# A decoder layer on one TensorE: end phase on plain loads, earlier operand loads, chores spread in steps, and POOL arithmetic moved to VectorE

## The chip, the cores and the metric

The kernel runs on one core of one Trainium2 chip. The metric is the device time of one launch in microseconds (us), as the median of several runs; a lower number is better. One further execution was recorded by the hardware profiler. Engines carry their short names: PE is TensorE (matmuls, and PEld its weight loads), DVE is VectorE, ACT is ScalarE, POOL is GpSimd, SP is SyncE, which only issues transfers. Each engine takes its instructions strictly in order.

## The reference, cut to what matters

One layer of width 1024 over 2048 positions, all in float32. One input projection gives six groups of 1024 columns; eight retention heads and four pooling windows use them, SiLU gates multiply both, and one output projection follows, with an RMSNorm before and one behind.

```python
h = rms_norm(x, pre_g)
proj = jnp.einsum('bsd,df->bsf', h, w_in)
q, k, v, g_ret, u, g_pool = jnp.split(proj, N_PROJ, axis=-1)
y_ret = retention_branch(q, k, v, positions, ret_norm_g) * jax.nn.silu(g_ret)
y_pool = pooling_branch(u, pool_w, pool_scale) * jax.nn.silu(g_pool)
y = jnp.concatenate([y_ret, y_pool], axis=-1)
y = jnp.einsum('bsf,fd->bsd', y, w_out)
return x + rms_norm(y, post_g)
```

Inside `retention_branch`, q and k are rotated by their position (`t1*cos - t2*sin`, `t1*sin + t2*cos`), then attention runs in chunks of 128 with a decaying state. `pooling_branch` takes running means over 2, 4, 8 and 16 positions and multiplies each group of 256 channels by `pool_w`.

## The kernel before, in words

**Products.** The large products are done by a 2x2 block scheme with seven block products instead of eight (sums S1 to S4 on the streamed side, made-up blocks on the resident side, and corrections on the result). Each float32 operand is split into an upper part (ACT, a copy that rounds) and a lower part (a subtraction), and three matmuls (upper x upper, upper x lower, lower x upper) stand for one. So one `Unit` is 7 products x 4 blocks x 3 = 84 matmuls of 128x512.

**Phases.** `line` lists 62 units in four phases: phase 0 the projections of rows 0 to 1023 (8 heads with a `qk` and a `vg` unit each, 8 `up` units for pooling), phase 1 the same for rows 1024 to 2047, phase 2 the first half of the output projection (`o0_0`, `o2_0`, ..., partial sums stored to the DRAM tensor `part`), phase 3, the end phase, its second half (`o0_8`, `o2_8`, ...), where `part` is added, the RMSNorm is taken, `x` is added and the rows go out. The first two units are written out by hand in `first`, which also takes the RMSNorm statistics of rows 0 to 1023 and builds the rotation tables.

**Order of the work.** A unit has seven steps (`at` 0 to 6, products 6, 2, 5, 7, 1 of the next unit, 4, 3). After each step `slot()` runs what `later(i, ...)` put i steps ahead, then a chore of the table `chores` starts if one stands at (phase, unit, step), and then the next unit's operands are prepared (`prep`) and the unit after that is loaded (`load`, at step 6). Chores are background work for later phases: `fold_pool_weights` (multiplies pool_w into the weights of `u`: operands split, 48 small matmuls, results stored), `stats_next`, `tables`, `combine_h` and `combine_o`. Within this program order the framework's scheduler settles each engine's queue.

**What the steps below touch.** A streamed load puts S1 and S3 in SBUF by a plain load from SP and an accumulating DMA from POOL on top of it, and the blocks 11, 12, 22 by plain loads (L254 to L268). `rope` (L420) rotates: two ACT copies swap the halves into `sw`, DVE multiplies by cos, POOL multiplies `sw` by sin (L431), DVE adds. `halves` (L753) splits the fold's operands with the lower part on POOL. In the end phase (`out_unit`) `total` copies or forms a result tile `ot`, adds `part` to it by an accumulating DMA from POOL (L686), squares it two steps later (L681), and `finish` normalises, adds `x` by an accumulating DMA (L732) and issues the store to `out` from SP (L733). Only the last unit fetches `part` by plain loads ahead (`fetch`, L673) and corrects with POOL (`adjust`, L677). Temporary tiles `T` (16 buffers of 128x528) are shared by all of this; streamed tiles `X` have 13 buffers.

Of the kernel before, what the change touches and what calls it, by code (L numbers as in the profile page):

```python
# [15 lines left out]
P = 128  # L16
# [65 lines left out]
def layer_kernel(ctx: ExitStack, tc: tile.TileContext, x, xt, pos, wt, wut, wo, pw, cols, postg, const, out):  # L82
# [126 lines left out]
    def combine_tile(n, j, b11, b12, b21, b22, keep):  # L209

        s = slice((j % 2) * BLK, (j % 2 + 1) * BLK)

        def put(p, t):
            nc.gpsimd.dma_start(out=made[n, p][j // 2][:, s], in_=t)

        def op(p, a, b, alu):
            t = T(f"c{n}{p}{j}")[:, :BLK]
            nc.vector.tensor_tensor(out=t, in0=a, in1=b, op=alu)
            put(p, t)
            return t  # L220
        if keep:
            for p, t in ((1, b11), (2, b21), (3, b22)):
                put(p, t)
        t1 = op(5, b11, b12, ALU.subtract)
        t2 = op(6, b22, t1, ALU.add)
        op(7, b12, b22, ALU.subtract)
        op(4, b21, t2, ALU.subtract)

    def combine_h(j, b0, b1):
# [4 lines left out]
        for name, b, k in (("b11", b0, j), ("b12", b1, j), ("b22", b1, KH + j), ("b21", b0, KH + j)):  # L234
            nc.vector.scalar_tensor_tensor(out=t[name], in0=t[name], scalar=col[:, k:k + 1], in1=rb[b],
                                           op0=ALU.mult, op1=ALU.mult)
        combine_tile(1, j, t["b11"], t["b12"], t["b21"], t["b22"], True)

    def combine_o(n, j):
# [5 lines left out]
        combine_tile(n, j, t["b11"], t["b12"], t["b21"], t["b22"], False)  # L245


    class Unit:
        def __init__(self, name, quads, uses):
            self.name, self.quads, self.uses = name, quads, uses  # L250
            self.op, self.bank = {}, {}
            self.fetch = self.adjust = None

        def load(self):  # L254
            self.raw = {}

            def land(name, q):
                t, view = X(f"{name}_{self.name}"), self.quads[q]
                dst = t if len(view.shape) == 2 else t.rearrange("p (f t) -> p f t", f=KH)
                nc.sync.dma_start(out=dst, in_=view)  # L260
                self.raw[name] = t
                return dst
            s1 = land("S1", "21")
            s3 = land("S3", "11")
            nc.gpsimd.dma_start(out=s1, in_=self.quads["22"], accum_op=ALU.add)
            nc.gpsimd.dma_start(out=s3, in_=self.quads["21"], accum_op=ALU.add)
            for q in ("11", "12", "22"):
                land(q, q)  # L268
# [11 lines left out]
        def prep(self, i):  # L280
            raw = self.raw
            if i == 0:
                self.add("S2", raw["S1"], raw["11"], nc.vector)
            elif i == 1:
                self.split(1, "11")
            elif i == 2:
# [10 lines left out]
            elif i == 8:  # L297
                self.split(3, "S4")

        def product(self, p, r):  # L300
# [20 lines left out]
            elif p == 6:  # L321
                nc.vector.tensor_tensor(out=o, in0=o, in1=self.x1, op=ALU.subtract)
                self.u2 = T(f"u2_{n}")[:, :BLK]
                nc.scalar.copy(out=self.u2, in_=o)  # L324
                if self.adjust:
                    self.adjust("12", self.u2)
            elif p == 2:
                self.uses["11"](o, True)
            elif p == 5:
                self.x5 = T(f"x5_{n}")[:, :BLK]  # L330
                nc.scalar.copy(out=self.x5, in_=o)
                if self.adjust:
                    self.adjust("22", self.x5)
# [21 lines left out]

    def stats_rows(b, tiles):
        ss = sml.tile([P, 2 * CPB], F32, name=f"ss{b}", tag="ss", bufs=4)
        for st in range(CPB):
            for j in range(2):
                r = tiles(st, j)  # L360
                nc.sync.dma_start(out=r, in_=x[b * BLK + st * P:b * BLK + (st + 1) * P, j * BLK:(j + 1) * BLK])
                nc.scalar.activation(out=r, in_=r, func=AF.Square, accum_out=ss[:, 2 * st + j:2 * st + j + 1])
        return ss

    def row_sums(b, ss):
        v = sml.tile([P, CPB], F32, name=f"rs{b}", tag="rs")
        s2 = ss.rearrange("p (s j) -> p s j", j=2)
        nc.vector.tensor_tensor(out=v, in0=s2[:, :, 0], in1=s2[:, :, 1], op=ALU.add)
        return v
# [30 lines left out]
    def tables(b):  # L400
        pi = T(f"pos{b}")[:, :BLK].bitcast(I32)
        nc.sync.dma_start(out=pi, in_=pos[:, b * BLK:(b + 1) * BLK].broadcast_to([P, BLK]))
        ang, kk = T(f"ang{b}")[:, :BLK], T(f"kk{b}")[:, :BLK]
        for step in angles(pi, ang, kk):
            step()
        cs, sn = T(f"cd{b}")[:, :BLK], T(f"sd{b}")[:, :BLK]
        nc.scalar.activation(out=sn, in_=ang, func=AF.Sin, scale=cst[:, C_SGN:C_SGN + 1])
        nc.scalar.activation(out=kk, in_=ang, func=AF.Abs)
        nc.scalar.activation(out=cs, in_=kk, func=AF.Sin, scale=-1.0, bias=cst[:, C_HPI:C_HPI + 1])
        for i, t in enumerate((cs, sn)):  # L410
            nc.gpsimd.dma_start(out=tabd[b][:, i, :], in_=t)
# [6 lines left out]
    held = []  # L418

    def rope(c, in_psum, b, name):  # L420
# [10 lines left out]
        nc.gpsimd.tensor_tensor(out=sw, in0=sw, in1=tabs[b][1], op=ALU.mult)  # L431
# [216 lines left out]
    def out_unit(s, f0, last, final=False):  # L648
# [26 lines left out]
        def adjust(q, t):  # L675

# [462 lines left out]
```

## Time and profile before

| what | value |
|---|---|
| median of 3 runs | 1624.98 us (1624.18 to 1631.08) |
| profiled execution, its own time | 1622.46 us |
| its span from first to last instruction | 1620.6 us |
| mean granted TensorE clock, share of full speed | 0.967 |
| PE / DVE / ACT / POOL busy, share of the span | 91% / 64% / 45% / 31% |
| DMA over the span | 243.80 MB, 150 GB/s on average |

The table gives averages over stages with different limits. The sections below read it stage by stage: in a stretch of the span, its length less PE's busy time is PE's idle time, and a granted clock under 1.00 says that part of the busy time ran at the lower of TensorE's two levels (1.2 instead of 2.4 GHz), where a matmul takes twice as long.

### The profile page before, as it was taken

The page shows a single profiled execution, that of the slowest core. Times are in us where ns is not written, and L with a number is a line of the kernel's source. Part 1 is how long each engine was busy: PE and PEld are TensorE (multiplying, and loading weights), DVE is VectorE, ACT ScalarE, POOL GpSimd, SP SyncE. Part 2 cuts the span into 40 slices and gives each one's busy share as a digit, 9 for nine tenths or more (in the row PEclk, how much of TensorE's full clock was granted, in tenths as well). Part 3 has the DMA queues.
Part 4 walks back from the last instruction along what each step waited for, and adds up shares of the span by engine and source line. Part 5 has one row for each costly group of instructions (what it writes and reads, how often), then busy time and mean ns, then how long its engine had stood idle before and what let it go on. Part 6 is the DMA issues. An engine that isn't in the chain of part 4 may idle for free. (4 is left out here: it accounts for less than half of the span.)

```text
span 1620.6 us, 20953 instructions
## 1 busy us (share of the span) xinstructions
PE 1473.8 (91%) x6976; PEld 1209.9 (75%) x6976; DVE 1044.2 (64%) x2166; ACT 722.6 (45%) x1383; POOL 500.0 (31%) x529
## 2 busy tenths in 40 slices
PE   4998979898989999799999999999996999987875
PEld 3777767687878888588888887887885888766664
DVE  6983736775757766876777667677677544645354
ACT  5554535445344434454444444344444433533331
POOL 0223231325252425522223314233245221133333
PEclk9999999999999999799999999999998999998987
DMA  8134544546454546544455535554456655887976
GB/s 309 41 78 124 150 111 109 151 131 173 140 155 133 162 123 173 180 116 105 117 156 149 161 82 148 144 162 108 121 153 191 177 155 144 286 194 149 221 163 175
DMA packets 115372, 243.80 MB, mean 150 GB/s; under 512 B 14016, under 2 KB 14144, under 8 KB 115264
## 3 DMA queue, kind: packets, MB, share of 16 engines
q1 hardware_dynamic: 75264, 149.12, 28.3%
q0 software_dynamic: 40000, 93.35, 26.4%
q8 instruction: 55, 0.90, 0.2%
q14 instruction: 53, 0.43, 0.1%
HBM read 187.88 MB, written 54.53 MB: 150 GB/s over the span
## 5 line engine op out<-in xcount | busy, mean ns | idle before, releaser
L312 PE MATMUL b_o<-rh,h_o 128*128 128x512 f32 x192 | 82.9, 432 | 40.3 <-ACT u_o L324 24.6
L431 POOL TENSOR_TENSOR sw_q<-sw_q,sin 128x512 f32<-128x512 f32 x32 | 50.6, 1583 | 144.7 <-ACT sw_q L429 98.8
L312 PE MATMUL b_up<-rh,h_up 128*128 128x512 f32 x192 | 78.7, 410 | 18.0 <-DVE gp L336 13.4
L443 POOL DMA_DIRECT2D yd<-sg x32 | 25.0, 780 | 196.3 <-DVE r L487 145.1
L312 PE MATMUL b_qk<-rh,h_qk 128*128 128x512 f32 x180 | 74.3, 413 | 10.7 <-DVE rot_k L336 5.6
L313 PE MATMUL b_o<-rl,h_o 128*128 128x512 f32 x192 | 81.2, 423 | 0.5 <-DVE rl L145 0.5
L314 PE MATMUL b_o<-rh,l_o 128*128 128x512 f32 x192 | 80.7, 420 | 0.0
L517 ACT ACTIVATE on<-op,sh,y_o 128x128 f32<-128x128 f32 x128 | 48.1, 456 | 72.7 <-DVE sh L514 72.7
L312 PEld LDWEIGHTS b_o<-rh,h_o 128*128 128x128 f32 x192 | 39.4, 205 | 54.8 <-ACT u_o L324 27.5
L313 PE MATMUL b_up<-rl,h_up 128*128 128x512 f32 x192 | 77.5, 404 | 0.0
L314 PE MATMUL b_up<-rh,l_up 128*128 128x512 f32 x192 | 77.4, 403 | 0.0
L313 PE MATMUL b_qk<-rl,h_qk 128*128 128x512 f32 x180 | 72.6, 403 | 0.0
L312 PE MATMUL b_vg<-rh,h_vg 128*128 128x512 f32 x180 | 72.3, 402 | 0.2 <-DVE rot_q L430 0.2
L314 PE MATMUL b_qk<-rh,l_qk 128*128 128x512 f32 x180 | 72.3, 402 | 0.0
L314 PE MATMUL b_vg<-rh,l_vg 128*128 128x512 f32 x180 | 70.5, 392 | 0.0
L313 PE MATMUL b_vg<-rl,h_vg 128*128 128x512 f32 x180 | 70.3, 391 | 0.0
L624 POOL TENSOR_TENSOR w<-ub 128x527 f32<-128x527 f32 x32 | 41.3, 1290 | 86.8 <-issue 41.1
L624 POOL TENSOR_TENSOR w<-w 128x525 f32<-128x525 f32 (+2 forms) x48 | 66.5, 1386 | 2.4
L145 DVE TENSOR_TENSOR rl<-m,rh 128x1024 fp32r<-128x1024 f32 x42 | 57.3, 1369 | 15.3 <-ACT rh L144 13.5
L431 POOL TENSOR_TENSOR sw_k<-sw_k,sin 128x512 f32<-128x512 f32 x32 | 49.8, 1557 | 56.1 <-ACT sw_k L429 53.0
L312 PEld LDWEIGHTS b_up<-rh,h_up 128*128 128x128 f32 x192 | 37.7, 197 | 28.8 <-DVE gp L336 15.3
L661 POOL DMA_DIRECT2D part<-pt_o x32 | 17.6, 552 | 108.9 <-ACT pt_o L349 65.7
(507 smaller groups left out, 4820.1 us busy)
## 6 DMA issues: line engine op xcount, KB each, us to landing
m<-made SPq DMA_DIRECT2D x30, 512.0 KB, 6.0
made<-c POOLq DMA_DIRECT2D x48, 256.0 KB, 4.0
yd<-sg POOLq DMA_DIRECT2D x32, 256.0 KB, 2.8
S_up<-in_wt POOLq DMA_DIRECT2D x32, 256.0 KB, 5.6
yd<-mx POOLq DMA_DIRECT2D x32, 256.0 KB, 2.8
b<-in_wo SPq DMA_DIRECT2D x32, 256.0 KB, 4.0
S_o<-yd SPq DMA_DIRECT2D x32, 256.0 KB, 4.0
S_o<-yd POOLq DMA_DIRECT2D x32, 256.0 KB, 5.9
```

Source lines behind the costliest of these rows:

```text
L145: (eng or nc.vector).tensor_tensor(out=r32(lo), in0=val, in1=hi, op=ALU.subtract)
L312: nc.tensor.matmul(o, wh, mh, start=opens and j == 0, stop=False, **more)
L313: nc.tensor.matmul(o, wh, ml, start=False, stop=False, **more)
L314: nc.tensor.matmul(o, wl, mh, start=False, stop=j == KH - 1, **more)
L431: nc.gpsimd.tensor_tensor(out=sw, in0=sw, in1=tabs[b][1], op=ALU.mult)
L443: nc.gpsimd.dma_start(out=yd[b][:, :, f, :], in_=t.rearrange("p (c t) -> p c t", c=CPB))
L517: nc.scalar.activation(out=self.on[:, c], in_=op[:, c], func=AF.Identity, scale=rs[:, i:i + 1], bias=shift[:, i:i + 1])
L624: nc.gpsimd.tensor_tensor(out=dst[:, s0:], in0=src[:, s0:], in1=src[:, s0 - step:E - step], op=ALU.add)
L661: nc.gpsimd.dma_start(out=place(part, q), in_=t)
```

## The change

- **End phase.** All eight units of phase 3 now do what the last one did: `fetch` loads their four quarters of `part` by plain loads on SP while the unit before runs. `taken` replaces the two ACT copies u2 and x5 by a DVE subtraction of `part`; the two results that come straight from PSUM get `part` by a DVE addition. The 28 accumulating DMAs from `part` and the two `adjust` steps on POOL are gone; the square is taken at once; the store to `out` is issued four steps after the accumulating DMA of `x`.
- **Streamed loads.** S1 and S3 are loaded at step 4, 11 and 22 at step 5, 12 at step 6, in place of all at step 6; the sum S2 = S1 + 11 moves from step 0 to step 1, behind the split of 11.
- **Chores.** `fold_pool_weights`, `stats_next`, `tables` and the `combine` chores issue their loads, splits, products and stores in separate steps (`later`), and the table places them elsewhere.
- **Beginning.** The first row tile of x is loaded first; the positions come as 128 full rows; the weights' upper and lower parts are split in separate steps.
- **From POOL to DVE.** The sin multiplication of the 64 rotations and the 20 lower parts of the folds.

```diff
     def combine_tile(n, j, src, keep):
...
+            t = src[p] = T(f"c{n}{p}{j}")[:, :BLK]
+            nc.vector.tensor_tensor(out=t, in0=src[a], in1=src[b], op=alu)
+            later(1, lambda: put(p, t))
...
+        def land(self, name, q, more=None):
+            t, view = X(f"{name}_{self.name}"), self.quads[q]
+            dst = t if len(view.shape) == 2 else t.rearrange("p (f t) -> p f t", f=KH)
+            nc.sync.dma_start(out=dst, in_=view)
+            if more:
+                nc.gpsimd.dma_start(out=dst, in_=self.quads[more], accum_op=ALU.add)
+            self.raw[name] = t
+
+        def load_sums(self):
+            self.raw = {}
+            self.land("S1", "21", "22")
+            self.land("S3", "11", "21")
...
         def prep(self, i):
             raw = self.raw
-            if i == 0:
-                self.add("S2", raw["S1"], raw["11"], nc.vector)
-            elif i == 1:
+            if i == 1:
+                h11 = raw["11"]
                 self.split(1, "11")
+                self.add("S2", raw["S1"], h11, nc.vector)
...
+        def taken(self, q, o, name):
+
+            t = T(f"{name}_{self.name}")[:, :BLK]
+            if self.part:
+                nc.vector.tensor_tensor(out=t, in0=o, in1=self.part[q], op=ALU.subtract)
+            else:
+                nc.scalar.copy(out=t, in_=o)
+            return t
...
-                self.u2 = T(f"u2_{n}")[:, :BLK]
-                nc.scalar.copy(out=self.u2, in_=o)
-                if self.adjust:
-                    self.adjust("12", self.u2)
+                self.u2 = self.taken("12", o, "u2")
...
-        nc.gpsimd.tensor_tensor(out=sw, in0=sw, in1=tabs[b][1], op=ALU.mult)
+        nc.vector.tensor_tensor(out=sw, in0=sw, in1=tabs[b][1], op=ALU.mult)
...
         def total(q):
-            def use(c, i):
-                o[q] = landed(c, i, f"ot{q}_{n}")
-                nc.gpsimd.dma_start(out=o[q], in_=place(part, q), accum_op=ALU.add)
...
-        def total_last(q):
             def use(c, i):
                 t = o[q] = T(f"ot{q}_{n}")[:, :BLK]
                 if i:
                     nc.vector.tensor_tensor(out=t, in0=c, in1=parts[q], op=ALU.add)
                 else:
                     c(t)
...
-                nc.sync.dma_start(out=out[spot], in_=t)
...
+                if final:
+                    nc.sync.dma_start(out=out[spot], in_=t)
+                else:
+                    later(4, lambda t=t, spot=spot: nc.sync.dma_start(out=out[spot], in_=t))
...
-        split(hi, lo, val, nc.gpsimd)
+        split(hi, lo, val)
...
     def fold_pool_weights(g):
-        pool = halves(f"p{g}", load_pool(g))
-        for dh in range(2):
-            fold_store(g, dh, fold_products(g, dh, pool, fold_split(g, dh, load_fold(g, dh))))
...
+        later(2, begin)
+        later(3, lambda: operands(0))
+        later(6, lambda: multiply(0))
+        later(7, lambda: fold_store(g, 0, st[0]))
+        later(7, second)
+        later(10, lambda: operands(1))
+        later(13, lambda: multiply(1))
+        later(14, lambda: fold_store(g, 1, st[1]))
...
             if i in upper:
                 split_w(*upper[i])
...
-    chores = {(0, 4, 0): lambda: fold_pool_weights(0), (0, 6, 0): lambda: fold_pool_weights(1),
-              (0, 12, 0): lambda: fold_pool_weights(2), (0, 15, 0): lambda: fold_pool_weights(3),
-              (0, 5, 0): lambda: stats_next(2), (0, 7, 0): lambda: stats_next(3),
-              (0, 8, 0): lambda: tables(2), (0, 9, 0): lambda: tables(3),
+    chores = {(0, 4, 0): lambda: fold_pool_weights(0), (0, 10, 0): lambda: fold_pool_weights(1),
+              (0, 14, 3): lambda: fold_pool_weights(2), (0, 16, 4): lambda: fold_pool_weights(3),
+              (0, 6, 0): lambda: stats_next(2), (0, 7, 3): lambda: stats_next(3),
+              (0, 12, 1): lambda: tables(2), (0, 13, 2): lambda: tables(3),
...
+    for j, u in enumerate(((8, 6), (18, 5), (19, 5), (20, 5))):
+        chores[(0, *u)] = lambda j=j: combine_h(j, 2, 3)
...
+                if n + 2 < len(line):
+                    ahead = line[n + 2][2]
+                    if at == 4:
+                        ahead.load_sums()
+                    elif at == 5:
+                        ahead.load_rest(("11", "22"))
+                    elif at == 6:
+                        ahead.load_rest(("12",))
```

**SP's queue in the end phase.** The first rows are those of before, from the middle of phase 3; `o4_8` runs, `o2_8` is the unit before it and `o8_8` the unit two ahead; `ot..` are its four results, `S1`, `S3`, `11`, `12`, `22` the streamed loads.

```order
L733 DMA out_0<-ot11_o2_8_13169 128x512
L733 DMA out_0<-ot22_o2_8_13241 128x512
L260 DMA S1_o8_8_13489<-yd2_91 128x512
L733 DMA out_0<-ot21_o2_8_13281 128x512
L733 DMA out_0<-ot12_o2_8_13302 128x512
L260 DMA S3_o8_8_13491<-yd2_91 128x512
L260 DMA 11_o8_8_13495<-yd2_91 128x512
L260 DMA 12_o8_8_13497<-yd2_91 128x512
L260 DMA 22_o8_8_13499<-yd2_91 128x512
```

The same place of the change, one unit earlier (`o2_8` runs, `o0_8` is before it, `o6_8` two ahead, `pt..` are the quarters of `part` for the next unit `o4_8`):

```order
L680 DMA pt11_o4_8_13265<-part4_97 128x512
L680 DMA pt22_o4_8_13267<-part5_98 128x512
L680 DMA pt21_o4_8_13269<-part5_98 128x512
L680 DMA pt12_o4_8_13271<-part4_97 128x512
L261 DMA S1_o6_8_13279<-yd1_90 128x512
L261 DMA S3_o6_8_13282<-yd1_90 128x512
L261 DMA 11_o6_8_13304<-yd1_90 128x512
L261 DMA 22_o6_8_13306<-yd1_90 128x512
L726 DMA out_0<-ot11_o0_8_13019 128x512
L726 DMA out_0<-ot22_o0_8_13065 128x512
L726 DMA out_0<-ot21_o0_8_13117 128x512
L726 DMA out_0<-ot12_o0_8_13140 128x512
```

S3, 11 and 22 stood behind the stores of the unit before; now they and S1 stand ahead of them, and only 12, the next row, stands behind. Four loads of `part` are new ahead of S1.

**POOL's queue in the end phase.** Before, one unit's stretch (`L686` adds `part`, `L732` adds `x`, `L265` and `L266` complete S1 and S3):

```order
L686 DMA ot22_o4_8_13425<-part5_98 128x512
L265 DMA S1_o8_8_13489<-yd2_91 128x512
L686 DMA ot21_o4_8_13465<-part5_98 128x512
L266 DMA S3_o8_8_13491<-yd2_91 128x512
L686 DMA ot12_o4_8_13486<-part4_97 128x512
L686 DMA ot11_o6_8_13537<-part6_99 128x512
L732 DMA ot11_o4_8_13353<-in_x 128x512
L732 DMA ot22_o4_8_13425<-in_x 128x512
L732 DMA ot21_o4_8_13465<-in_x 128x512
L732 DMA ot12_o4_8_13486<-in_x 128x512
```

The change:

```order
L722 DMA ot11_o2_8_13177<-in_x 128x512
L722 DMA ot22_o2_8_13245<-in_x 128x512
L722 DMA ot21_o2_8_13297<-in_x 128x512
L722 DMA ot12_o2_8_13320<-in_x 128x512
L263 DMA S1_o8_8_13463<-yd2_91 128x512
L263 DMA S3_o8_8_13466<-yd2_91 128x512
```

A unit has six accumulating transfers where it had ten, and no result of the running unit stands ahead of S1 and S3 any more.

**PE's queue at a fold.** Before, the third fold's first products (`p2h`, `p2l` the parts of pool_w, `w200..`, `w201..` those of the weights; `a_vg5_0` belongs to a unit):

```order
L774 MATMUL wf2_01_3529<-p2l_3501,w200h_3508 128x256
L775 MATMUL wf2_00_3516<-p2h_3500,w200l_3509 128x256
L775 MATMUL wf2_01_3529<-p2h_3500,w200l_3509 128x256
L312 MATMUL a_vg5_0_3674<-b11h0_271,h1_vg5_0_3625 128x512
L313 MATMUL a_vg5_0_3674<-b11l0_273,h1_vg5_0_3625 128x512
L773 MATMUL wf2_00_3516<-p2h_3500,w201h_3512 128x256
```

The change, the same fold:

```order
L764 MATMUL wf2_00_4233<-p2h_4129,w200h_4151 128x256
L765 MATMUL wf2_00_4233<-p2l_4130,w200h_4151 128x256
L766 MATMUL wf2_00_4233<-p2h_4129,w200l_4152 128x256
L764 MATMUL wf2_00_4233<-p2h_4129,w201h_4155 128x256
L765 MATMUL wf2_00_4233<-p2l_4130,w201h_4155 128x256
L766 MATMUL wf2_00_4233<-p2h_4129,w201l_4156 128x256
```

The fold's products stood in pieces as their operands were made, with unit matmuls between; now each result's twelve stand in one run.

## Rows read from the trace of the kernel before

**Rows 1.** The page's first part: busy us, share, instructions of each engine.

```profile
PE 1473.8 (91%) x6976; PEld 1209.9 (75%) x6976; DVE 1044.2 (64%) x2166; ACT 722.6 (45%) x1383; POOL 500.0 (31%) x529
```

**Rows 2.** Stretches of the span: length, busy per engine (x), PEclk, DMA share, GB/s.

```profile
0.00:40.00 40.00, 18.63 (x61) 12.20 (x62) 25.97 (x63) 21.96 (x39) 0.20 (x4) 1.00 0.84 313
40.00:100.00 60.00, 56.95 (x270) 46.08 (x269) 56.82 (x87) 33.58 (x53) 13.42 (x11) 1.00 0.24 51
...
140.00:265.00 125.00, 109.98 (x565) 90.53 (x565) 63.72 (x164) 62.88 (x137) 38.33 (x38) 0.95 0.47 129
265.00:485.00 220.00, 202.68 (x1011) 168.03 (x1010) 143.51 (x328) 98.83 (x197) 78.27 (x83) 0.98 0.51 144
485.00:637.00 152.00, 149.86 (x743) 125.13 (x742) 109.06 (x231) 66.93 (x135) 53.90 (x59) 1.00 0.49 138
637.00:718.00 81.00, 69.44 (x291) 55.77 (x290) 64.44 (x76) 40.31 (x67) 37.70 (x31) 0.89 0.61 178
718.00:1186.00 468.00, 460.43 (x2329) 385.62 (x2328) 321.30 (x742) 211.10 (x405) 138.16 (x146) 1.00 0.49 130
1186.00:1264.00 78.00, 63.91 (x260) 50.74 (x259) 59.76 (x71) 36.95 (x66) 36.58 (x34) 0.91 0.61 184
1264.00:1378.00 114.00, 114.00 (x503) 94.10 (x502) 49.69 (x75) 43.30 (x74) 22.46 (x35) 1.00 0.56 154
...
1421.00:1607.00 186.00, 151.42 (x587) 119.35 (x585) 82.59 (x186) 61.87 (x136) 60.34 (x68) 0.90 0.81 182
```

**Rows 3.** Waits in 1421:1607: who for whom, us in total, times, longest.

```profile
DVE sS_o L272 <- DMA S_o<-yd: 46.2, 6, 10.3
```

**Rows 4.** DMA queues and issues in 1421:1607: share of 16 engines; us to landing.

```profile
q0 software_dynamic: 9648, 17.57, 56.5%
q1 hardware_dynamic: 8851, 16.12, 23.8%
...
ot_o<-in_x POOLq DMA_DIRECT2D x28, 256.0 KB, 5.8
out<-ot_o SPq DMA_DIRECT2D x28, 256.0 KB, 5.2
ot_o<-part POOLq DMA_DIRECT2D x26, 256.0 KB, 6.4
S_o<-yd POOLq DMA_DIRECT2D x12, 256.0 KB, 5.7
S_o<-yd SPq DMA_DIRECT2D x10, 256.0 KB, 5.1
```

**Rows 5.** One stretch of 20 us where phase 2 meets phase 3.

```profile
1380.00:1400.00 20.00, 17.87 (x78) 14.15 (x77) 13.41 (x17) 10.74 (x17) 3.95 (x6) 1.00 0.94 307
```

**Rows 6.** PE's waits over the whole span.

```profile
PE c_qk L312 <- ACT x_qk L331: 9.7, 4, 4.4
...
PE wf L773 <- ACT w110h L144: 4.2, 1, 4.2
PE f L935 <- DVE b21l L922: 3.8, 4, 1.8
PE wf L775 <- POOL w110l L145: 3.6, 1, 3.6
```

**Rows 7.** The rotations' POOL line L431: duration min/median/max in ns, and who waited.

```profile
L431 POOL TENSOR_TENSOR sw_q<-sw_q,sin x32: 1267/1632/2318, 40.6 to 1144.2; 128x512 f32<-128x512 f32 x32
...
  DVE rot_k L433: 17.8, 19
  DVE rot_q L433: 11.3, 21
```

**Rows 8.** Timeline of POOL and DVE near 1230: start, us, instruction.

```profile
1225.94 4.55 POOL L624 TENSOR_TENSOR w<-w 128x525 f32<-128x525 f32 x3
1226.34 1.54 DVE L145 TENSOR_TENSOR l_o<-sS_o,h_o 128x512 fp32r<-128x512 f32 x1
...
1237.98 0.69 DVE L145 TENSOR_TENSOR l_o<-S_o,h_o 128x512 fp32r<-128x512 f32 x1 [4.07 <-ACT h_o L144]
```

**Rows 9.** Timeline of DVE at the start of phase 1.

```profile
645.81 0.69 DVE L272 TENSOR_TENSOR sS_qk<-S_qk,11_qk 128x512 f32<-128x512 f32 x1 [4.45 <-DMA S_qk<-in_wt]
```

More of the change, by code (lines that the diff above doesn't have):

```diff
@@ L216, in op @@
         def op(p, a, b, alu):
[L217 to L220, printed above, removed]
+            t = src[p] = T(f"c{n}{p}{j}")[:, :BLK]
+            nc.vector.tensor_tensor(out=t, in0=src[a], in1=src[b], op=alu)
+            later(1, lambda: put(p, t))
         if keep:
[L222 to L227, printed above, removed]
+            for p, name in ((1, "b11"), (2, "b21"), (3, "b22")):
+                later(5, lambda p=p, name=name: put(p, src[name]))
+        d = 5 if keep else 3
+        later(d, lambda: op(5, "b11", "b12", ALU.subtract))
+        later(d, lambda: op(6, "b22", 5, ALU.add))
+        later(d + 1, lambda: op(7, "b12", "b22", ALU.subtract))
+        later(d + 1, lambda: op(4, "b21", 6, ALU.subtract))
     def combine_h(j, b0, b1):
@@ L233, in combine_h, with scaled @@
             nc.sync.dma_start(out=t[name], in_=xt[b, k // 2][:, (k % 2) * BLK:(k % 2 + 1) * BLK])
[L234 to L237, printed above, removed]
+        def scaled(part):
+            for name, b, k in part:
+                nc.vector.scalar_tensor_tensor(out=t[name], in0=t[name], scalar=col[:, k:k + 1], in1=rb[b],
+                                               op0=ALU.mult, op1=ALU.mult)
+        later(3, lambda: scaled((("b11", b0, j), ("b12", b1, j))))
+        later(4, lambda: scaled((("b22", b1, KH + j), ("b21", b0, KH + j))))
+        combine_tile(1, j, t, True)
     def combine_o(n, j):
@@ L251, in __init__, with load_rest @@
             self.op, self.bank = {}, {}
-            self.fetch = self.adjust = None
-        def load(self):
[L255 to L268, printed above, removed]
+            self.fetch = self.part = None
+        def land(self, name, q, more=None):
[9 more added lines that the diff above has]
+            self.land("S3", "11", "21")
+        def load_rest(self, names):
+            for q in names:
+                self.land(q, q)
+        def load(self):
+            self.load_sums()
+            self.load_rest(("11", "22", "12"))
         def add(self, k, a, b, eng):
@@ L353, in landed @@
         return t
[L356 to L369, printed above, removed]
     def scale_h(b, ss, n=CPB):
@@ L400, in tables, with turn, trig, keep @@
     def tables(b):
[L401 to L411, printed above, removed]
+        pi, ang, kk = T(f"pos{b}")[:, :BLK].bitcast(I32), T(f"ang{b}")[:, :BLK], T(f"kk{b}")[:, :BLK]
+        nc.sync.dma_start(out=pi, in_=pos[:, b * BLK:(b + 1) * BLK])
+        steps = angles(pi, ang, kk)
+        def turn(part):
+            for step in part:
+                step()
+        def trig():
+            cs, sn = T(f"cd{b}")[:, :BLK], T(f"sd{b}")[:, :BLK]
+            nc.scalar.activation(out=sn, in_=ang, func=AF.Sin, scale=cst[:, C_SGN:C_SGN + 1])
+            nc.scalar.activation(out=kk, in_=ang, func=AF.Abs)
+            nc.scalar.activation(out=cs, in_=kk, func=AF.Sin, scale=-1.0, bias=cst[:, C_HPI:C_HPI + 1])
+            later(1, lambda: keep(cs, sn))
+        def keep(cs, sn):
+            for i, t in enumerate((cs, sn)):
+                nc.gpsimd.dma_start(out=tabd[b][:, i, :], in_=t)
+        for i in range(4):
+            later(2 + i, lambda i=i: turn(steps[2 * i:2 * i + 2]))
+        later(7, trig)
     def fetch_tables(b):
@@ L840, in load, with row @@
             return t
-        def rows(b):
-            return [load(wide(f"xs{b}{st}"), x[b * BLK + st * P:b * BLK + (st + 1) * P, :]) for st in range(CPB)]
+        def row(b, st):
+            return load(wide(f"xs{b}{st}"), x[b * BLK + st * P:b * BLK + (st + 1) * P, :])
         def square(b, st, t):
@@ L877, in load_pi @@
             pi[b] = T(f"pos{b}")[:, :BLK].bitcast(I32)
-            nc.sync.dma_start(out=pi[b], in_=pos[:, b * BLK:(b + 1) * BLK].broadcast_to([P, BLK]))
+            nc.sync.dma_start(out=pi[b], in_=pos[:, b * BLK:(b + 1) * BLK])
+        xs = {0: [row(0, 0)]}
         nc.sync.dma_start(out=cst, in_=const)
         load_pi(0)
-        xs = {0: rows(0)}
+        xs[0] += [row(0, st) for st in range(1, CPB)]
         nc.sync.dma_start(out=col, in_=cols)
@@ L897, in first @@
                 load_w(k, q)
-        xs[1] = rows(1)
+        xs[1] = [row(1, st) for st in range(CPB)]
         load_pi(1)
```

96 lines of the change are left out of this document (54 added, 42 removed).

## Prediction

> **What bounds the kernel now.** First the page's busy times: PE 1473.8 us of 1620.6, DVE 64%, POOL 31% [rows 1]. PE is the bound, but its busy time also holds slow matmuls, so the second view is the table of stretches [rows 2]. The reader should look there for the one clean stretch: in 1264:1378 PE is busy for all of 114.00 us, at clock 1.00, with 503 matmuls, so 0.227 us each and 19.05 us for a unit of 84. Against that, the idle time (length less PE busy) by stretch: 0:40 21.4 us, 40:100 3.1, 140:485 15.0 + 17.3 = 32.3 (the chores of phase 0), 637:718 11.6 (phase 0 to 1), 718:1186 7.6, 1186:1264 14.1 (phase 1 to 2), 1421:1607 34.6 (the end phase). Stretches with stalls also show a clock under 1.00: a mean of 0.90 over 186 us means that a fifth of it ran at the lower level of 1.2 GHz. So a stall costs twice, and the end phase and the chores hold most of it. Third, the waits name what ends the idle time: in the end phase DVE waits 46.2 us for the streamed sums S_o to land [rows 3], and what stands behind in DVE's queue is what empties PSUM for PE; in the chores it is ACT's x_qk (9.7 us) and the folds' operands (4.2 and 3.6 in one fold) [rows 6].
>
> **The change, part by part.** The sum is made against the profiled execution's 1622.5 us, which lies 2.5 us under the median.
>
> *End phase, -35.5 us.* In 1421:1607, 587 matmuls are 7.0 units, so 26.6 us a unit against 19.05 clean. What may it come to? The DMA engines give one limit. POOL's queue q0 moved 17.57 MB, 67 transfers of 256 KB, in 56.5% of 186 us: 1.57 us of all 16 engines each, nearly all accumulating. SP's q1 moved 16.12 MB, 61.5 transfers, in 23.8%: 0.72 us each [rows 4]. A unit of before has 10 accumulating and 9 plain transfers (22.2 us, 0.83 of the 26.6, as the row's share of 0.81 says); the new one has 6 and 13: 9.4 + 9.4 = 18.8 us. So the engines would be 99% busy if PE ran clean, and the nearest stretch with such a load, 1380:1400 at a share of 0.94, lost 2.1 of 20 us on PE [rows 5]. I take 21.5 us a unit, by that row: 7.0 x (26.6 - 21.5) = 35.5. Bounds: 19.05 (gain 53) and no gain. The wait for S_o should go because of the order: S3, 11, 22 no longer stand behind stores that wait for accumulating transfers, and on POOL S1 and S3 are no longer behind transfers for results that PE has yet to make. The four loads of `part` stand ahead of S1 on SP; each waits for a T buffer that the stores of two units ago free, which is the new thing that could be late (below). DVE gets four more instructions of 0.69 us a unit: 82.6 us busy over 7 units become some 102 of 150, still beside PE; ACT loses four copies.
>
> *Chores and folds, -28 us.* 140:485 is 345 us with 32.3 idle. At the rate of the stretches without folds (485:637 and 718:1186: 9.7 of 620 us) it would be 5.4, so 26.9 idle are due to the chores. The clock of 0.95 and 0.98 puts 12.5 and 8.8 us at the lower level, half of it lost: 10.7. Together 37.6 us can be had. The folds' products stood in PE's queue ahead of units while their operands were still being loaded, copied and subtracted on POOL (L431's like takes 1.3 us and more [rows 7]; a DVE subtraction of 128x512 takes 0.69 [rows 8]). Now loads stand 3 steps, lower parts 3 steps (about 8 us) ahead of the products, and ACT's copies come singly, so x_qk is no longer behind a bunch of them. I take three quarters, since the steps still share ACT and DVE with units. Bounds -38 and 0. The 20 lower parts are 13.8 us more on DVE, which is busy 207 of 345 us there.
>
> *Rotations, 0 us away from the start.* 64 x 0.69 = 44.2 us go to DVE. It gets back the 29.1 us for which it waited for POOL before the adding [rows 7]; the net 15 lies beside PE, since DVE is busy 69% of 718:1186. If that cover were gone, it costs 15, or 44 with nothing given back. There may be a gain: a DVE instruction with two SBUF inputs took 1.54 us while POOL's L624 ran, 0.69 alone [rows 8], and the rotations' POOL time of 1.3 to 2.3 us each is such a neighbour. I take nothing for it, since which instructions met a rotation isn't in one row.
>
> The Trainium skill, "SBUF — State Buffer", § Who interferes with whom, says that a DVE instruction with two SBUF inputs and a GpSimd instruction that reads SBUF block each other in full; the pair of rows agrees, and by that rule the move gives DVE back time on every such meeting and rival C gets likelier.
>
> *Phase changes, -8 us.* At the start of phase 1 DVE waits 4.45 us for S_qk [rows 9], and a PE stall follows; the loads now start two steps earlier and the sum is taken a step later. I take 5 there, 3 for the like into phase 2. The rest is DVE itself (64.4 of 81 and 59.8 of 78 us busy, with 14 lower parts of 128x1024 for the next phase), which stays. Bounds -20 (all idle time but 6) and +6, the rotations of a unit pair exposed twice.
>
> *Beginning, -1 us.* The four waits for b21l [rows 6] are 3.8 us: DVE stood before a weight's lower part until ACT had copied its upper one; that comes a step later now. With the first rows sooner I take -4. Against it 4 rotations of 0.69 fall into 40:100, where DVE is busy 56.8 of 60 us, +3. Bounds -6 and +4.
>
> *New waits, +4 us.* Chores cut into steps keep T buffers for longer, and each engine waits in order for a buffer. No row shows it; between 0 and 15 (the DVE net above exposed) I take a value near the lower end, as 718:1186 has chores and units at 1.6% idle.
>
> Sum: 1622.5 - 35.5 - 28 - 8 - 1 + 4 = 1554; with the offset to the median 1554 to 1556.5, so 1555.
>
> **Rivals.**
>
> *A. The transfers, not their queue, hold the end phase.* The bytes of `part` are the same; if the accumulating form isn't what made q0's transfers dear (q0's 1.57 us could be the queue's own cost under load), a unit stays at 26.6 us and 35.5 are lost: 1590. For it: DMA share of 0.81 already, 0.94 beside a PE loss. Against it: q1's 0.72 us in the same 186 us. Chance 0.14.
>
> The Trainium skill, "DMA: Bandwidth & Descriptors", § Issuing engines are not separate DMA queues, says that transfers from all engines share the same 16 DMA engines, and another issuer saves its issue time only; taken alone it speaks for A.
>
> *B. DVE becomes the bound in phases 0 and 1.* Its 58 us more fall where PE waits for PSUM to be emptied: the chores' gain is lost (+28) and the rotations' net 15 shows: 1598. For it: 95% busy in 40:100, 80% in 637:718. Against: 51 to 72% elsewhere. Chance 0.12.
>
> *C. All of it is covered.* End phase at 19.5 us a unit (-50), chores -38, phase changes -16, beginning -4, no new waits: 1515. For it: the clean 1264:1378. Chance 0.11.
>
> *D. Slower: SP's queue becomes a ring.* Loads of `part` wait for the stores of two units ago, those for the accumulating `x`; behind them stand S1 and S3 and then their accumulation. These are four landings in a row, 5.8 + 5.2 + 5.1 + 5.7 = 21.8 us [rows 4], in the 13 steps between `finish` and the use of S, 1.86 unit times. At 21.5 us that is 40 us, so 18 are left for all else. If landings double under the load, 61.6 / 1.86 = 33.1 us a unit: 1622.5 + 46 - 33 = 1635. It decides from landings of 1.8 times today's on; below that the unit stays under 31.3 us and the other parts win. Chance 0.05.
>
> *E. Chores and loads moved without effect,* and the end phase gains a third only: within 8 us of before. Chance 0.03.
>
> **How the numbers follow.** The forecast, 1530 to 1580, has 0.55; A 0.14, B 0.12, C 0.11, D 0.05, E 0.03. The range of 8 in 10 takes all of the forecast, most of C and A and the nearer half of B: 1518 to 1598. A change under 0.5% (8 us) is about what a measurement of this kernel can't tell from none: faster by more 0.90, within 0.05 (E and the edges of B), slower 0.05.
>
> **What would show it.** In the changed profile: the end phase's units at 20 to 22 us, DVE's wait for S_o under 10 us, PE's clock there over 0.95, a DMA share over 0.9, and q0's and q1's cost per transfer still about 1.6 and 0.7 (A would show q1 dearer). PE's idle time in the chores under 15 us, no wait for `wf` operands over 1 us. DVE's busy time up by 58 us or less; by clearly less if POOL had been slowing it. POOL's busy time down by about 130 us. The forecast is wrong if SP's loads of `part` are late (DVE waiting for `pt` or `12`), if DVE's busy share passes 90% in any stretch of phase 0 with PE idle behind it, or if the folds' waits only change their name.

## The result, and the profile after

The changed kernel takes 1511.5 us (median of 4 runs, 1509.2 to 1515.7) against 1628.0 (4 runs beside it): a ratio of 0.928, 95% interval 0.924 to 0.932. The forecast was 1555 us with a low end of 1518: the sign is right, and the time lies 6.5 us under that end. The two profiled executions are 112.6 us apart where the sum had 68.5, so 44 us have to be accounted for.

The page's first part, as in [rows 1]:

```profile
PE 1436.5 (95%) x6976; PEld 1194.8 (79%) x6976; DVE 1077.0 (71%) x2280; ACT 709.6 (47%) x1353; POOL 349.3 (23%) x415
```

PE does the same 6976 matmuls in 37.3 us less busy time. DVE has 114 more instructions and only 32.8 us more.

To see where the 112.6 us between the two spans (1620.6 and 1508.0) came from, the span is cut where PE has done the same units. Stretches of before, cut so (columns as in [rows 2], but of the engines only PE): units 1 to 20 with the chores, phase 0 to 1, phase 1, phase 1 to 2, and the last eight units.

```profile
98.80:637.30 538.50, 500.60 (x2527) 0.98 0.49 136
637.30:718.10 80.80, 69.24 (x290) 0.89 0.61 178
718.10:1186.30 468.20, 460.63 (x2330) 1.00 0.49 130
1186.30:1263.70 77.40, 63.31 (x257) 0.91 0.61 184
1400.00:1606.50 206.50, 171.09 (x673) 0.91 0.81 187
```

The same units after; here PE's busy time is followed by that of PEld, DVE, ACT and POOL:

```profile
94.20:578.20 484.00, 481.50 (x2519) 407.63 (x2518) 362.76 (x861) 247.05 (x505) 109.71 (x139) 1.00 0.54 150
578.20:654.20 76.00, 67.79 (x289) 53.69 (x288) 60.10 (x79) 39.74 (x66) 31.46 (x28) 0.93 0.62 188
654.20:1112.90 458.70, 456.45 (x2330) 385.07 (x2329) 333.16 (x771) 211.78 (x405) 94.95 (x118) 1.00 0.49 134
1112.90:1187.60 74.70, 62.66 (x257) 49.55 (x256) 51.88 (x69) 36.00 (x65) 36.72 (x33) 0.93 0.59 181
1321.40:1492.30 170.90, 158.96 (x673) 129.12 (x671) 113.73 (x235) 63.53 (x129) 36.96 (x43) 0.96 0.86 228
```

Length against length: the beginning -4.6 us (98.8 to 94.2), units 1 to 20 -54.5, the phase changes -4.8 and -2.7, phase 1 -9.5, the last eight units -35.6 and the unit ahead of them -2.5; the tail is 1.6 longer. Before, PE was idle for 37.9 us in the chores' stretch, and it was busy 19.1 us longer than after for nearly the same matmuls; after, 2.5 us are idle at a clock of 1.00. Nothing else in the kernel gave so much.

PE's waits in that stretch after (94.2:578.2) are all of these:

```profile
PE b_up L330 <- ACT u_up L315: 1.1, 1, 1.1
PE b_up L330 <- DVE gp L348: 1.0, 2, 0.8
PE vt L477 <- DVE vT L354: 0.2, 1, 0.2
```

Neither `x_qk` nor `wf` of [rows 6] is left. In the last eight units (1321.4:1492.3) DVE's waits for streamed sums, and in 1340:1500 the two DMA queues, as in [rows 3, 4]:

```profile
DVE sS_o L281 <- DMA S_o<-yd: 8.7, 4, 2.7
...
DVE sS_o L281 <- DMA 12_o<-yd: 4.1, 3, 2.6
```

```profile
q1 hardware_dynamic: 13449, 24.53, 44.2%
q0 software_dynamic: 5760, 10.49, 40.4%
```

A transfer of 256 KB cost q0 1.62 us of all 16 engines (40.0 in 64.6 us) and q1 0.76 (93.6 in 70.7): their prices held, and fewer of the dear ones are made.

### The profile page after: what moved, and what is told of

It reads as the page before. It is cut to its first block, busy times and chain, and to the rows that moved or that the text cites. A ratio compares the mean times of both kernels' runs of the same rounds, so it can differ in the third digit from the quotient of the medians.

```text
span 1508.0 us, 20797 instructions
## 1 busy us (share of the span) xinstructions
PE 1436.5 (95%) x6976; PEld 1194.8 (79%) x6976; DVE 1077.0 (71%) x2280; ACT 709.6 (47%) x1353; POOL 349.3 (23%) x415
## 4 chain that ended last, share of the span: by engine, by line
PE 44%; DVE 5%; issue 5%; DMA 4%; POOL 3%; ACT 1%; SPq 1%; POOLq 0%; DVEq 0%; ACTq 0%
POOL w L631 2%; DMA S_o<-yd 2%; PE b_o L330 2%; PE b_o L331 2%; PE b_up L330 2%; PE b_o L332 2%; PE b_up L331 2%; PE b_up L332 2%; PE b_vg L332 1%; PE b_vg L330 1%; PE b_vg L331 1%; PE b_qk L330 1%; PE b_qk L331 1%; PE b_qk L332 1%; PE c_o L330 1%
## 5 line engine op out<-in xcount | busy, mean ns | idle before, releaser
L330 PE MATMUL b_o<-rh,h_o 128*128 128x512 f32 x192 | 78.2, 407 | 13.5 <-DVE ot_o L348 9.2
L331 PE MATMUL b_o<-rl,h_o 128*128 128x512 f32 x192 | 77.3, 403 | 0.0
L332 PE MATMUL b_o<-rh,l_o 128*128 128x512 f32 x192 | 76.9, 401 | 0.0
L263 POOL DMA_DIRECT2D S_qk<-in_wt x30 | 26.5, 907 | 174.0 <-DMA S_qk<-in_wt 114.6
L145 DVE TENSOR_TENSOR rl<-m,rh 128x1024 fp32r<-128x1024 f32 x42 | 53.0, 1265 | 19.1 <-ACT rh L144 16.4
L330 PEld LDWEIGHTS b_up<-rh,h_up 128*128 128x128 f32 x192 | 37.3, 194 | 24.5 <-DVE gp L348 10.0
L263 POOL DMA_DIRECT2D S_vg<-in_wt x30 | 26.6, 910 | 129.9 <-DMA S_vg<-in_wt 54.2
L330 PE MATMUL a_o<-rh,h_o 128*128 128x512 f32 x128 | 49.9, 390 | 2.8 <-ACT x_o L338 2.8
```

Source lines behind the costliest of these rows:

```text
L145: (eng or nc.vector).tensor_tensor(out=r32(lo), in0=val, in1=hi, op=ALU.subtract)
L263: nc.gpsimd.dma_start(out=dst, in_=self.quads[more], accum_op=ALU.add)
L330: nc.tensor.matmul(o, wh, mh, start=opens and j == 0, stop=False, **more)
L331: nc.tensor.matmul(o, wh, ml, start=False, stop=False, **more)
L332: nc.tensor.matmul(o, wl, mh, start=False, stop=j == KH - 1, **more)
```

## The experiments

The theories at the start: **S**, the spacing of the chores gave what the forecast missed; **P**, POOL's arithmetic had slowed DVE and ACT; **L**, the earlier streamed loads carry the gain. Each kernel is the changed one with an edit, unless said otherwise. Beside each of the three groups of four the kernel before ran again (medians 1627.8, 1629.3, 1632.3 us), so ratios to it are compared too; the changed kernel didn't run beside them.

**1. POOL's arithmetic back.**

```diff
-        nc.vector.tensor_tensor(out=sw, in0=sw, in1=tabs[b][1], op=ALU.mult)
+        nc.gpsimd.tensor_tensor(out=sw, in0=sw, in1=tabs[b][1], op=ALU.mult)
...
-        split(hi, lo, val)
+        split(hi, lo, val, nc.gpsimd)
```

> The changed kernel with only the POOL-to-DVE move undone: the 64 sin multiplications and the 20 lower parts of the folds are on POOL again. Theory S (spacing): the time that the chores lost was lost because their products stood in PE's queue ahead of units whose operands were not made, and because ACT copied in bunches; who subtracts matters little, since the products now stand three steps behind. Then 1511 to 1520 us, and PE's idle time in the chores stays under 15 us. Theory P (POOL as neighbour): the forecast missed 44 us mostly because POOL's elementwise work slowed DVE and ACT; the DVE time above its undisturbed durations fell from 76 us before to 42 after. Then at least half of those 34 us come back on the path, 1528 us or more.

Measured: 1524.8 us, ratio 0.937 (0.933 to 0.940). So 13 us of the gain is the move to DVE: more than S allowed, less than P asked. Its page:

```profile
PE 1440.7 (94%) x6976; PEld 1193.5 (78%) x6976; DVE 1064.9 (70%) x2196; ACT 708.1 (46%) x1353; POOL 474.4 (31%) x499
```

84 instructions of 0.69 us are 58 us of DVE work; without them DVE is busy only 12.1 us less. The other 46 come back as slower DVE instructions; by the single durations of the trace, added up, it is 35. (Busy time counts once where one instruction starts before the last one's end.)

**2. The chores back,** bodies and table.

```diff
     def fold_pool_weights(g):
...
-        later(2, begin)
-        later(3, lambda: operands(0))
...
+        pool = halves(f"p{g}", load_pool(g))
+        for dh in range(2):
+            fold_store(g, dh, fold_products(g, dh, pool, fold_split(g, dh, load_fold(g, dh))))
...
-    chores = {(0, 4, 0): lambda: fold_pool_weights(0), (0, 10, 0): lambda: fold_pool_weights(1),
+    chores = {(0, 4, 0): lambda: fold_pool_weights(0), (0, 6, 0): lambda: fold_pool_weights(1),
...
```

> The changed kernel with only the chores undone: fold_pool_weights, stats_next, tables and combine issue all their work at once again, at the places of the table of before; all else, the move to DVE too, stays. Theory S: units 1 to 20 lost 61 us before and 4 after, and nearly all of that returns, 1555 to 1570 us, with waits of PE for the folds' operands of over 1 us again. Theory P: less than half of it returns, 1511 to 1535 us. If the early loads carried it (theory L), also under 1535.

Measured: 1557.2 us, ratio 0.957 (0.953 to 0.961), 46 us lost, as S expects. Units 1 to 20 and phase 1 of this kernel:

```profile
94.20:621.40 527.20, 498.84 (x2519) 415.17 (x2518) 365.23 (x861) 247.82 (x505) 110.74 (x141) 0.98 0.50 139
695.70:1162.10 466.40, 458.88 (x2330) 386.11 (x2329) 336.39 (x772) 212.23 (x405) 95.95 (x118) 1.00 0.49 131
```

Units 1 to 20 are 43.2 us longer, 25.9 of it idle and 17.3 in the busy time of 2519 matmuls in both, at a clock of 0.98; phase 1 is 7.7 us longer. PE's first waits in 94.2:621.4 are those of before again:

```profile
PE c_qk L326 <- ACT x_qk L311: 10.0, 4, 4.6
PE wf L765 <- ACT w110h L144: 4.5, 1, 4.5
PE b_qk L326 <- ACT ub L616: 3.0, 1, 3.0
```

**3. The streamed loads back:** all at step 6, S2 at step 0.

```diff
-            if i == 1:
-                h11 = raw["11"]
+            if i == 0:
+                self.add("S2", raw["S1"], raw["11"], nc.vector)
...
-                    if at == 4:
-                        ahead.load_sums()
-                    elif at == 5:
-                        ahead.load_rest(("11", "22"))
...
+                elif n + 2 < len(line):
+                    line[n + 2][2].load()
```

> The changed kernel with only the streamed loads undone: all five loads and both accumulations at step 6, S2 taken at step 0 of the next unit. Theories S and P: the phase changes gained 7 us and phase 1 gained 9.5, and only these return at most, 1514 to 1528 us; the end phase keeps 21 to 22 us a unit. Theory L (the early loads carry the gain, in the end phase too, since S1 and S3 then stand ahead of what the unit stores): 1535 us or more, with DVE waiting for S_o again.

Measured: 1554.6 us, ratio 0.955 (0.951 to 0.958). L is right about 43 us, and the largest piece is in the end phase, 195.6 us against 170.9 for its eight units, though its transfers are the new ones. The stretch, DVE's waits in it, and PE's first wait:

```profile
1341.80:1537.40 195.60, 165.83 (x673) 132.87 (x671) 113.32 (x234) 63.82 (x130) 37.99 (x44) 0.93 0.76 199
```

```profile
DVE sS_o L276 <- DMA S_o<-yd: 31.5, 5, 9.3
...
DVE sS_o L276 <- issue: 7.4, 1, 7.4
```

```profile
PE a_o L327 <- DVE l_o L145: 18.6, 5, 6.9
```

PE waits for the lower parts that DVE makes behind the late sum; after, no such wait stands in this stretch.

Another 11.2 us are in units 1 to 20, where loads had played no part in the forecast (495.2 against 484.0).

**4. The end phase back,** early loads kept.

```diff
         def total(q):
+            def use(c, i):
+                o[q] = landed(c, i, f"ot{q}_{n}")
+                nc.gpsimd.dma_start(out=o[q], in_=place(part, q), accum_op=ALU.add)
...
-                    later(4, lambda t=t, spot=spot: nc.sync.dma_start(out=out[spot], in_=t))
...
+                    nc.sync.dma_start(out=out[spot], in_=t)
```

> The changed kernel with only the end phase undone: the 28 accumulating transfers of part are back, with the four plain loads gone, the square two steps later, the store to out at once; loads stay early. If the accumulating transfers made the end phase dear, as the prediction has it: 26 to 27 us a unit, 1545 to 1555 us. If the early loads of S1, S3, 11 and 22 were what helped there (theory L): 22 to 23 us a unit, under 1525 us.

Measured: 1545.2 us, ratio 0.950 (0.947 to 0.953). The eight units take 210.7 us, 26.3 each (206.5 before): early loads alone give the end phase nothing. PE's first waits in 1320:1531 are on result tiles and copies, not on loads; behind them ACT waits for the accumulated `part` before it can square:

```profile
PE b_o L330 <- DVE ot_o L348: 24.1, 6, 7.3
PE b_o L330 <- ACT u_o L315: 11.3, 5, 4.0
```

```profile
ACT sq_o L684 <- DMA ot_o<-part: 30.2, 11, 4.3
```

**5. Only the folds spaced:** `stats_next`, `tables` and `combine` issue at once, at the new places.

```diff
-    def combine_tile(n, j, src, keep):
+    def combine_tile(n, j, b11, b12, b21, b22, keep):
...
-            later(1, lambda: put(p, t))
...
+            put(p, t)
```

> The changed kernel with stats_next, tables and combine issuing all their work at once again, at the new places; the folds of pool_w stay spaced, and so does the table. Undoing all chores and their table cost 46 us. If the folds carried that (their products stand in PE's queue, the others' work doesn't), 1511 to 1522 us. If the bunches of ACT and DVE work in the others carried it, 1535 us or more.

Measured: 1527.9 us, ratio 0.937 (0.935 to 0.940): 14 to 16 us lost, between both bounds. So of the 46 us, some 30 are by difference due to the folds with the table, the rest to the other chores; no run has the folds alone undone. Their part shows in both phases: units 1 to 20 take 495.5 us (+11.5) and phase 1, which has `combine_o` alone, 465.3 (+6.6).

```profile
662.20:1127.50 465.30, 457.31 (x2330) 384.98 (x2329) 336.65 (x771) 212.40 (x405) 95.12 (x118) 1.00 0.49 132
```

**6. The kernel before with the new end phase alone.**

```diff
-                self.u2 = T(f"u2_{n}")[:, :BLK]
-                nc.scalar.copy(out=self.u2, in_=o)
-                if self.adjust:
-                    self.adjust("12", self.u2)
+                self.u2 = self.taken("12", o, "u2")
...
         def total(q):
-            def use(c, i):
-                o[q] = landed(c, i, f"ot{q}_{n}")
-                nc.gpsimd.dma_start(out=o[q], in_=place(part, q), accum_op=ALU.add)
...
-        def total_last(q):
             def use(c, i):
                 t = o[q] = T(f"ot{q}_{n}")[:, :BLK]
```

> The kernel before with the new end phase alone: part by plain loads, no accumulation of it, the store of out four steps later; streamed loads, chores and POOL as before. Theory C (both are needed: fewer accumulations and loads two steps earlier, since the changed kernel with late loads had 24.5 us a unit in the end phase and with the old accumulations 26.3): 24 to 25 us a unit, a gain of 8 to 18 us on the kernel before. If the plain transfers suffice, as the prediction has it (21.5 us a unit), a gain of 35 us.

Measured: 1619.4 us, ratio 0.993 (0.991 to 0.996), a gain of 10 us. The eight units take 195.0 us, as in experiment 3, and DVE waits for S_o:

```profile
1408.40:1603.40 195.00, 166.76 (x673) 132.97 (x671) 113.36 (x234) 63.51 (x130) 37.95 (x44) 0.92 0.77 198
```

```profile
DVE sS_o L272 <- DMA S_o<-yd: 31.5, 5, 9.0
```

Theory C of this expectation holds: plain transfers alone are worth 11.5 us there, early loads alone nothing, both together 35.6.

**7. Only S1 and S3 early.**

```diff
-                    elif at == 5:
-                        ahead.load_rest(("11", "22"))
                     elif at == 6:
-                        ahead.load_rest(("12",))
+                        ahead.load_rest(("11", "22", "12"))
```

> The changed kernel with S1 and S3 loaded at step 4 as it is, but 11, 22 and 12 all at step 6 again; S2 still taken at step 1. If the sums, with their two transfers one after the other, are what was late (DVE waited 25 us for S_o with all loads at step 6), the end phase stays at 21 to 22 us a unit and the whole at 1511 to 1520 us. If the plain blocks' time matters as much, 1530 us or more, with DVE waiting for 11_o or 12_o in the place of S_o.

Measured: 1514.5 us, ratio 0.929 (0.927 to 0.931), 1 to 3 us lost, within the noise. The sums, two transfers one behind the other, are what had to start earlier, not the plain blocks, whose part in the profile is 6.6 us: the eight units take 177.5. S2 is still taken at step 1 here, a step later than in experiments 3 and 6; what that step is worth by itself was not tested.

**8. All streamed loads one step earlier still.**

```diff
-                    if at == 4:
+                    if at == 3:
                         ahead.load_sums()
+                    elif at == 4:
+                        ahead.load_rest(("11", "22"))
                     elif at == 5:
...
```

> The changed kernel with all streamed loads one step earlier still (S1 and S3 at step 3, 11 and 22 at 4, 12 at 5). In the changed kernel's end phase DVE still waits 8.7 us for S_o and 3.5 for 12_o. If landing is what is late, those go, the end phase comes to 20 us a unit or less, and the whole to 1498 to 1506 us. If the loads then wait for a free buffer, or the DMA engines are full (their share is 0.86 there), nothing changes: 1507 to 1516 us.

Measured: 1508.5 us, ratio 0.926 (0.923 to 0.928). DVE's wait for S_o halves, and the end phase doesn't move (169.3 us, share 0.86). The first expectation fell. But the waits for transfers moved rather than went: in the eight units DVE waits for others (`out`, `m`, `pt`) for 6.5 us in all where it had waited 4.1 for 12_o, and ACT for 11_o 15.6 us where it had waited 1.6.

```profile
DVE sS_o L281 <- DMA S_o<-yd: 4.1, 4, 1.7
```

**9 and 10. The two halves of experiment 1:** its first pair of lines alone, and its second pair alone.

> The changed kernel with only the 64 sin multiplications of the rotations on POOL again; the folds' lower parts stay on DVE. Both together cost 13 us, with DVE's busy time only 12 us lower for 58 us of work less. If POOL's presence beside DVE is what costs (the rotations are 101 us of POOL's time, the lower parts 28), nearly all returns: 1519 to 1526 us. If the price lies in the folds' chain of operands (PE waits 1.4 us for a lower part from POOL), 1510 to 1516 us.

> The changed kernel with only the 20 lower parts of the folds on POOL again; the rotations stay on DVE. By POOL's presence beside DVE: 1511 to 1516 us, the rest of the 13 us. By the folds' chain of operands: 1519 to 1526 us.

Measured beside each other: 1519.7 us (ratio 0.931, 0.928 to 0.933) with the rotations on POOL, 1512.2 (0.926, 0.923 to 0.928) with the lower parts there. So the rotations cost 7.5 us more than the lower parts; against the changed kernel they cost 8 us by time and 4 by ratio, within the noise of the ratios. The halves don't add up to the whole: units 1 to 20 grow by 5.6 and 2.7 us, and by 13.2 in experiment 1. Pages of both:

```profile
PE 1441.1 (95%) x6976; PEld 1196.6 (79%) x6976; DVE 1059.8 (70%) x2216; ACT 708.8 (47%) x1353; POOL 448.9 (30%) x479
```

```profile
PE 1435.2 (95%) x6976; PEld 1192.7 (79%) x6976; DVE 1078.2 (72%) x2260; ACT 710.5 (47%) x1353; POOL 376.6 (25%) x435
```

64 instructions, 44.2 us by the row of 0.69, make DVE's busy time 17.2 us longer, so 27.0 are given back (18.2 by the single durations). The 20 lower parts on DVE leave its busy time as it was, so nearly all of their 13.8 us is given back (11.6 by the single durations), and yet the time of the kernel stays. One meeting, in the timeline of the first near 283 (start, us, instruction): POOL multiplies, and DVE's L437, whose median is 0.69 us, takes 1.78 and ends 0.55 us after POOL:

```profile
282.25 0.68 DVE L218 TENSOR_TENSOR c<-b,b 128x512 f32<-128x512 f32 x1
...
283.21 1.47 POOL L438 TENSOR_TENSOR sw_q<-sw_q,sin 128x512 f32<-128x512 f32 x1 [1.23 <-ACT sw_q L436]
...
283.45 1.78 DVE L437 TENSOR_TENSOR rot_q<-rot_q,cos 128x512 f32<-128x512 f32 x1
```

A second cost of a rotation on POOL is that it comes out later. With it there, DVE waits 29.8 us for POOL's products, and PE for the finished rotation (no such wait after):

```profile
PE kt L463 <- DVE rot_k L440: 3.3, 4, 1.0
```

Which of the two costs the kernel its time isn't separated.

**11 and 12. Two further versions of experiment 8:** the four scalings of a finished row pair spread over steps (`scaled` stands for the loop in `finish`), and the same with `x` loaded plainly and added by POOL (one quarter in four by DVE). The stores to `out` follow the scaling by three steps in the first and by one in the second.

```diff
+                scaled(quads[:1])
+                for i in range(1, 4):
+                    later((i + 1) // 2, lambda i=i: scaled(quads[i:i + 1]))
```

```diff
-                    nc.gpsimd.dma_start(out=t, in_=x[spot], accum_op=ALU.add)
...
+                    if True:
+                        xr = T(f"xr{q}_{n}")[:, :BLK]
+                        nc.sync.dma_start(out=xr, in_=x[spot])
...
+                        eng = nc.vector if q == "12" else nc.gpsimd
+                        eng.tensor_tensor(out=t, in0=t, in1=xr, op=ALU.add)
```

> A further version: the loads one step earlier still, and in the end phase the four scalings of a finished row pair (4 x 0.69 us on DVE in one piece, behind which DVE's next result for PE stood) put one, two and one to a step, each followed by its accumulating transfer of x. If DVE's order is what PE still waits for there (9.2 us for ot_o, and for ACT behind it), the end phase comes to 20 us a unit or less, 1495 to 1504 us in all. If the DMA engines at a share of 0.86 hold it, 1505 to 1514 us.

> The same as the scalings spread, and x too is loaded by plain transfers on SP and added by POOL in all eight end units, in the place of the 28 accumulating transfers. If accumulating transfers' engine time (1.6 us against 0.7) still holds the end phase, it comes to 19.5 us a unit and the whole to 1492 to 1502 us. If POOL's additions beside DVE cost as the rotations did there, no gain on the kernel with the scalings spread, or a loss of up to 8 us.

Measured beside each other: 1509.0 us (ratio 0.924, 0.921 to 0.928), the same as experiment 8 within the intervals; and 1518.8 (0.930, 0.928 to 0.932), 10 us worse than its neighbour. In the second the DMA share fell, and the eight units still grew to 178.5 us:

```profile
1321.90:1500.40 178.50, 159.68 (x672) 127.99 (x671) 126.54 (x242) 62.96 (x129) 42.30 (x36) 0.97 0.71 222
```

So DVE's order at the scaling isn't what holds the last 17 to 18 us that the eight units lose against the clean 152.4 (8 x 19.05). Whether the DMA engines' load does, the second doesn't tell, since it brings new waits of its own. DVE's busy time there is 126.5 us against 115.2 in experiment 11, with seven instructions more (242 to 235), and DVE waits for POOL's additions and for x:

```profile
DVE ot_o L686 <- POOL ot_o L721: 19.7, 5, 5.6
DVE ot_o L721 <- DMA xr_o<-in_x: 16.1, 6, 3.8
```

## Why the prediction was right or wrong, step by step

**Chores and folds, -28: the step that failed.** The stretch gave 54.5 us, 35.4 of idle time and 19.1 of busy time. The step took 26.9 us of idle time and 10.7 of clock, 37.6 in all, and three quarters of that; the bound of 38 on the gain was itself too low. Three things made it so.

- Idle time, 8.5 us more. Of these 5.6 lie outside 140:485, to which the step kept (3.4 in 100:140 and 2.1 in 485:637.3, rounded). The rest is the 5.4 us that it left standing at the rate of 485:637 and 718:1186, where only 2.5 stayed: those stretches weren't clean, since they held `combine` chores, which the change spreads too.
- Busy time, 8.4 us more. The step priced only the lower clock, and not wrongly: 23.9 us of the stretch ran at 1.2 GHz, PE was busy for 19.0 of them, and half of that is 9.5. Some 6 us more are an estimate for the stops themselves: PE's busy time stands in 44 pieces before and in 7 after, and a matmul of 128x512 is shown for 0.39 us at the end of a piece, where in a run the next one follows after 0.23. The other 4 us or less (8 matmuls fewer are about 1) stay open.
- The withheld quarter, 9.4 us, came in full.

The mechanism was right: the signs that were named came (2.5 us idle, no wait on `wf`), and with the bodies and the table undone, `x_qk` and `wf` are back, and 43.2 us in that stretch. The undone parts overlap: chores 43.2, POOL's arithmetic 13.2 (497.2 us in experiment 1) and loads 11.2 make 67.6 of 54.5, so each hides some of the others' work.

**Rotations, 0.** The net 15 us beside PE was harmless, but "I take nothing for it" was wrong: the rotations alone are some 4 to 8 us of the gain (experiment 9, hardly clear of the noise), and 13 with the folds' lower parts (experiment 1). DVE got back 18 to 27 of 44.2 us in instructions that no longer meet POOL, and its busy time rose by 32.8 us, clearly less than 58, the sign that was named for it. The rule on mutual blocking that was weighed there (the Trainium skill, "SBUF — State Buffer", § Who interferes with whom) agrees with the row of 1.78 us above. The row of 1.54 us in [rows 8] was ground enough for a term. That DVE's time is what gained is not shown: the lower parts gave DVE theirs back and gained nothing by themselves, and the shorter way to a finished rotation is a second cause.

**End phase, -35.5.** Right in size: 35.6 us for eight units, 21.2 us for each of the last seven (forecast 21.5), prices of q0 and q1 as forecast, S_o at 8.7 us (under 10 forecast), clock 0.96, share 0.86 (over 0.9 forecast). The size was in part luck: 21.5 was taken from a row with a share of 0.94, which didn't come, and what does hold the units at 21.2 is open (experiments 8, 11 and 12). The cause was told only by half. The step let S_o's wait go "because of the order" and priced the transfers, without saying that two edits make this order; with the accumulating transfers gone and the loads late, 24.4 us a unit and a wait of 31.5 us remain (experiments 3 and 6). The sums' earlier start was needed as well. The plain blocks' was not (experiment 7), and how much of it is the later S2 is open. Rival A, with the transfers themselves as the limit, falls, since the queue's price held and the unit shrank. Of the signs of being wrong one showed, if small: DVE waited 4.1 us for `12` (none for `pt`).

**Phase changes, -8:** 7.5 measured. Idle time there is still 8.2 and 12.0 us.

**Beginning, -1:** -4.6; the +3 for rotations between 40 and 100 didn't show.

**New waits, +4, and phase 1, which the sum left at 0:** no new wait shows among PE's in the stretches above, and phase 1 gave 9.5 us. Of these 7.7 return with the chores (experiment 2) and 6.6 with `combine_o` in one piece (experiment 5): a stretch that idled for only 1.6% still had bunches of chores to spread.

The sum of the miss: 26.5 for the chores, 9.5 for phase 1, 4 for waits that didn't come, 3.6 at the beginning, 2.6 at the unit ahead of the end phase and in it, less 0.5 at the phase changes and 1.6 in the tail, makes 44. Rival C named this direction at a chance of 0.11 and 1515 us, but by an end phase (19.5 us a unit) that didn't come and with chores at 38. Rivals B, D and E fell: DVE's busy share is 75% in the chores (362.8 of 484.0) and 79% at the phase 0 to 1 change; only in 40:94.2 does it pass 90% (52.5 of 54.2 us), with PE idle for 1.1 us.

## What to carry to other kernels

A "clean rate" taken from the same kernel has to be free of the thing that is being removed; here the fair measure was the busy time and idle time of the same matmuls, unit by unit. Where a stall has two causes in a row (a crowded queue and a late start), undoing one shows little (11.5 us and nothing, of 35.6), so a term for two edits belongs to the pair. And an operation moved from POOL to DVE is priced net of the DVE instructions that it had been holding up.

## What the runs showed of the hardware beyond the forecast

A rotation on POOL of 1.47 us made a neighbouring DVE instruction take 1.78 instead of 0.69 us; over 64 rotations that was 18 to 27 us of DVE time, and 20 subtractions moved from POOL left DVE's busy time at 1077.0 us against 1078.2. A transfer of 256 KB on POOL's queue, where nearly all accumulate, cost 1.62 us of all 16 engines, and 0.76 on SP's, where all are plain. With `x` on plain transfers too, the end phase's DMA share fell from 0.86 to 0.71, and the kernel became 10 us slower as DVE came to wait for POOL's additions and for x; what the engines' load costs there by itself isn't shown.
